# Second convolution product into FFN: a fixed order on every engine, two units' first products side by side, the sample's norms last

## The chip, the cores and the metric

The kernel runs on one core of a Trainium2 chip. The metric is the device time of one execution in microseconds (us).

## The reference, cut to what matters

One layer of an encoder, the same weights for a prompt of 1024 rows and a sample of 256 rows, all fp32, model width 1024, FFN width 2816:

```python
h = rms_norm(x, norms[0])
b, c, v = split(h @ conv_w_in, 3)
mix = (b * conv3(c * v)) @ conv_w_out        # the second product of the convolution
x = x + rms_norm(mix, norms[1])              # norm 1 and the residual
h = rms_norm(x, norms[2])                    # norm 2
gate, up = split(h @ ffn_w_in, 2)
x = x + rms_norm((silu(gate) * up) @ ffn_w_out, norms[3])
```

## The kernel before, in words

**Arithmetic.** A matrix product in fp32 is made of three products of parts in fp32r: each operand is split into a high part (ScalarE, a copy that rounds) and a low part (VectorE, operand minus high part), and high x high, high x low and low x high are summed in PSUM (`TERMS`, `product`, L200). On top, the prompt's part of a product is done with Strassen-like sums of 2 x 2 blocks: seven block products of 12 matmuls each instead of eight.

**Stages.** First the input product of the convolution (12 units), then the second product, here called mm2 (weights `w2t`, result tiles `mx`), then FFN-in (22 units F0, F1, ..., each of 128 gate and 128 up columns), then FFN-out (weights `w4`). The 1280 rows make ten tiles of 128, 0 to 7 of the prompt and 8 and 9 of the sample; mm2 takes them in the order 0, 4, 1, 5, 2, 6, 3, 7, 8, 9.

**After a tile of mm2** (`after_mm2`, L683): ScalarE squares the two halves with a running sum, VectorE and GpSimd make the factor of norm 1, VectorE scales the two halves, adds the residual (`x1`), SP stores `x1` to DRAM, then the same again for norm 2 (squares, factor, one scaling into `ht`). Two tiles later TensorE transposes `ht` in two halves of four 128 x 128 blocks (`transposes`, L650). Prompt tiles go into the quadrants a11, a12, a21, a22 (`ar`), sample tiles are split into `hs`, high part on ScalarE and low part on VectorE.

**Operands of FFN-in.** `early_sums` (L711) splits a11 and forms the block sums (a21 + a22, then a11 minus that, then s3) for a range of columns; `make_c` splits a12, s1 (the a21 sum), s2 (the a11 sum), s3, a22 and s4 (a12 plus the a11 sum). A unit's weights are loaded as 1 MB (`load`, L162) and split as `g`, `u`, then `sums`, `t13`, `t24` (`make`, L177). A unit (`Block`, L210) does its block products in the order x: a11 with g; y: a12 with g; x: s2 with t24; z: s1 with t13; x: s3 with t13; the sample's two products (24 matmuls of 256 columns each); x: a22 with t24; z: s4 with u. The bank x is added to and read out several times, each time before its next product. `EvF` (L809) holds what is read out, its SiLU and the product with the up part.

**What sets the order.** Up to the end of FFN-in the instructions are put in order by the framework's scheduler, which follows the program's order as priority and runs ahead where operands and places are free. Here, F0's and F1's first instructions and the norms of tiles 8 and 9 are all in its hands. FFN-out is under `tc.manual_schedule()` (L1247): there each engine keeps the order in which the program names the instructions, chosen by a planner written out in the kernel (`fill`, `advance`, clocks in us for each engine, `row_free` for the time from which a buffer row is free). `load_w4` (L912) asks for the next 1 MB of FFN-out weights, into a place of pool `b` or into two rows of the pools `a` and `s`; `load_units` (L1042) asks for the activation tiles (`ut`, and the small ones `us` that the `yo` product reads). All of these loads, and the stores of `spill`, go out on SP's queue in order, and a load that must wait for its place holds those behind it. PSUM has eight banks, taken in turn.

Of the kernel before, what the change touches and what calls it, by code (L numbers as in the profile page):

```python
# [8 lines left out]
F32 = mybir.dt.float32  # L9
# [27 lines left out]
def encoder_kernel(ctx: ExitStack, tc: tile.TileContext, xT, x, g0T, gB, cwT, w1, w2, w3, w4, out_p, out_s):  # L37
# [3 lines left out]
    const = ctx.enter_context(tc.tile_pool(name="const", bufs=1))  # L41
    tmp = ctx.enter_context(tc.tile_pool(name="tmp", bufs=3))
    mem = ctx.enter_context(tc.tile_pool(name="mem", bufs=1))
    ps = ctx.enter_context(tc.tile_pool(name="ps", bufs=8, space=PS))
    dram = ctx.enter_context(tc.tile_pool(name="dram", bufs=1, space=bass.MemoryType.DRAM))


# [57 lines left out]
    def copy(out, a):  # L105
        nc.scalar.activation(out, a, AF.Copy)  # L106

    def new_ps(name):
        return ps.tile([P, 512], F32, tag="mm", name=name)

    def new_tmp(name):
        return tmp.tile([P, 512], F32, tag="ta", name=name, bufs=6)
# [9 lines left out]
    def sumsq(parts, name, i=None):  # L122

        acc = small(2, name)
        for h, src in enumerate(parts):
            junk = new_tmp(f"j_{name}_{h}")
            nc.scalar.activation(junk, src, AF.Square, accum_out=acc[:, h : h + 1])
        tot = small(1, name + "t")
        if i is None:
            add(tot, acc[:, 0:1], acc[:, 1:2])  # L130
        else:
            nc.vector.scalar_tensor_tensor(
                out=tot, in0=acc[:, 0:1], scalar=acc[:, 1:2], in1=rq[:, i : i + 1], op0=ALU.add, op1=ALU.mult
            )
        rstd(tot, tot, 1)
        if i is not None:
            nc.gpsimd.tensor_tensor(out=tot, in0=tot, in1=rt[:, i : i + 1], op=ALU.mult)
        return tot

    def halves(ap):  # L140
        return [ap[:, :H], ap[:, H:]]
# [502 lines left out]
    for i in (0, 1):  # L644
        nc.sync.dma_start(gb[:, i], gB[i].partition_broadcast(P))
    ar = {(kh, c): get(f"ar{kh}{c}", [KH, 512]) for kh in (0, 1) for c in (0, 1)}
    hs[:] = [get(f"hs{p}", [KD, 256], F32R) for p in "hl"]
    hts, mx = {}, {}

    def transposes(i):  # L650
        for q in range(2):
            o = new_ps(f"tr{i}_{q}")
            for k in range(4):
                nc.tensor.transpose(
                    o[:, k * P : (k + 1) * P], hts[i][:, (4 * q + k) * P : (4 * q + k + 1) * P], ident
                )
            ov = o.rearrange("p (k t) -> p k t", k=4)
            if i < 8:
                t0 = i % 4 * P
                dst = ar[q, i // 4][:, :, t0 : t0 + P]  # L660
                if q:
                    nc.vector.tensor_copy(dst, ov)
                else:
                    copy(dst, ov)
            else:
                t0 = (i - 8) * P
                split(*(h[:, 4 * q : 4 * q + 4, t0 : t0 + P] for h in hs), ov)
        put(hts.pop(i))

    def mm2(*tiles, ks=range(KD)):  # L670
        for i in tiles:
            if i not in mx:
                mx[i] = [new_ps(f"mx{i}_{h}") for h in range(2)]
# [9 lines left out]
    def after_mm2(i):  # L683
        put(zs.pop(i))
        xt = xts.pop(i)
        o = mx.pop(i)
        r = sumsq(o, f"n1_{i}", i)
        x1 = get(f"x1_{i}", [D], kind="a")
        for h in range(2):
            sl = slice(h * H, (h + 1) * H)  # L690
            nc.vector.scalar_tensor_tensor(
                out=x1[:, sl], in0=o[h], scalar=r, in1=gb[:, 0, sl], op0=ALU.mult, op1=ALU.mult
            )
        add(x1, x1, xt)
        put(xt)
        nc.sync.dma_start(x1d[i], x1)
        r = sumsq(halves(x1), f"n2_{i}")
        hts[i] = get(f"ht{i}", [D], kind="s")
        nc.vector.scalar_tensor_tensor(out=hts[i], in0=x1, scalar=r, in1=gb[:, 1], op0=ALU.mult, op1=ALU.mult)
        put(x1)  # L700

    xts = {}

# [17 lines left out]
        load_z(i, KD - 2, KD)  # L721
    for i in ORDER2[:2]:
        load_xt(i)
    for n, i in enumerate(ORDER2):
        last = n == NT - 1
        if n == 0:
            mm2(i, ORDER2[1])
        elif n > 1:
            if n == 8:
                load_z(ORDER2[9])  # L730
                cb["a11"] = [get(f"a11{p}", [KH, 512], F32R) for p in "hl"]
                s3 = get("s3", [KH, 512])
                early_sums(slice(0, 3 * P))
            early = KD - 2 if n < 4 else 1
            mm2(i, ks=range(early))
            transposes(ORDER2[n - 2])
            if last:
                early_sums(slice(3 * P, 4 * P))
            mm2(i, ks=range(early, KH))
            if last:  # L740
                put(*w2t[:KH])
                make_c("a12", a12)
                add(a12, a12, a11)
                make(F0, "t24")
                make_c("s2", a11)
                put(a11)
            mm2(i, ks=range(max(early, KH), KD))
        if last:
            put(*w2t[KH:])
        after_mm2(i)  # L750
        if n and not last:
            if n != 8:
                load_z(ORDER2[n + 1])
            load_xt(ORDER2[n + 1])
        if n == 4:
            load(F0)
            for what in ("g", "u", "sums"):
                make(F0, what)
    make(F0, "t13")
    make_c("s1", a21)  # L760
    put(a21)
    make_c("s3", s3)
    put(s3)


    A11, S1, S2, S4, A12, S3, A22 = range(7)
# [42 lines left out]
    class EvF:  # L809


        def __init__(self, f):
            self.f = f
            self.a = act[f] = get(f"act{f}", [2, HALF], kind="a")

        def tmp(self, q):
            return new_tmp(f"{q}{self.f}_")
# [4 lines left out]

        def add11(self, y):
            add(self.c11, self.c11, y)
            nc.scalar.activation(self.c11, self.c11, AF.Silu)

        def read12(self, x):
# [1 line left out]
            copy(self.c12, x)  # L829

        def read22(self, x, z):
            self.c22 = self.tmp("c22")
            copy(self.c22, x)
            add(self.c22, self.c22, z)

        def read21(self, x):
            g2 = self.tmp("g2")
            nc.scalar.activation(g2, x, AF.Silu)
            mul(prompt(self.a, 1), g2, self.c22)

        def add12(self, z):
            add(self.c12, self.c12, z)
# [7 lines left out]
        def end(self):  # L850
            pass

    def ffn_in(f):
        units = [("f", g) if g < KF else None for g in (f, f + 1, f + 2)]
        if f:
            b = Block(units[0], EvF(f), *units[1:], final=f == KF - 1)
            b.p12()
            b.p657()
            b.sample()
            b.p43()  # L860
        else:
# [12 lines left out]
            b.p657(after6)  # L874
            transposes(ORDER2[-2])
            transposes(ORDER2[-1])
            put(gb)
            make(F1, "u")
            make(F1, "sums")
            b.p43(lambda: make(F1, "t13"))  # L880
            b.sample()
            make(F1, "t24")
            load(F2)
        if f % 2 and f < KF - 1:
            for _ in spill(f // 2):
                pass
# [25 lines left out]
    def load_w4():  # L912
# [21 lines left out]
    def weights():  # L934

        for gi, grp in enumerate(GROUPS):
            for jn, j in enumerate(grp):
# [135 lines left out]
    def advance(entry, limit):  # L1073
# [2 lines left out]
            return False  # L1076
        ready = ready() if callable(ready) else ready or 0.0
        if rows:
            tags = (free["s"] + free["a"])[:rows]
            ready = max([ready] + [row_free.get(tag, 0.0) for tag in tags])  # L1080
        done = max(clock[engine], ready) + cost
        if done > limit:
            return False
# [249 lines left out]
```

## Time and profile before

| | us |
|---|---|
| median of 3 runs | 1273.21 (1272.68 to 1274.07) |
| the profiled execution | 1271.61 |
| its span, first to last instruction | 1269.8 |
| TensorE busy | 1242.1 (98%) |
| VectorE busy | 841.0 (66%) |
| ScalarE busy | 466.4 (37%) |
| mean granted TensorE clock | 0.993 of full |

The profiled execution's time is 1.8 us more than its span: what lies before the first and after the last instruction. Busy shares are means over all stages; a matmul counts as busy until its modelled end, so neighbours overlap. mm2 runs from 323.5 to 440.1 us, FFN-in from there to 996.0, FFN-out after that.

### The profile page before, as it was taken

The numbers are of one execution on the slowest core, as the hardware profiler recorded it, in microseconds if no ns is written. First come the engines' busy times: TensorE is split into PE (matmuls) and PEld (weight loads), VectorE is DVE, ScalarE is ACT, GpSimd is POOL, SyncE is SP. The second block draws the span as 40 slices with busy tenths as digits, with TensorE's granted clock in tenths as the row PEclk, the third lists the DMA queues.
The fourth block names the chain that finished last, engine by engine and source line by source line (L and its number), as shares of the span: only waits on it lengthen the run. The fifth ranks groups of instructions, "written<-read, shape, count | busy, mean of one in ns | idle before, by whom it ended". The sixth has DMA issues, their size and how long they took to land.

```text
span 1269.8 us, 15906 instructions
## 1 busy us (share of the span) xinstructions
PE 1242.1 (98%) x6213; PEld 1052.6 (83%) x6213; DVE 841.0 (66%) x1177; ACT 466.4 (37%) x694; POOL 26.5 (2%) x49
## 2 busy tenths in 40 slices
PE   8899999999999989999999999999999999999997
PEld 6688888888888868888888888888888878788885
DVE  7996655757265786565664755755657478769566
ACT  7743332325133554333343433433434342112011
POOL 0100000000011100000000000000000000000000
PEclk9899999999999999999999999999999999999999
DMA  7504041225953213452552642634626788866894
GB/s 266 165 34 149 34 117 54 87 92 175 336 204 124 103 49 109 129 170 97 157 158 87 178 128 85 189 113 120 191 86 196 268 284 295 277 225 209 284 331 176
DMA packets 185595, 207.37 MB, mean 163 GB/s; under 512 B 7984, under 2 KB 145584, under 8 KB 184496
## 3 DMA queue, kind: packets, MB, share of 16 engines
q1 hardware_dynamic: 185088, 205.83, 50.0%
q8 instruction: 49, 0.80, 0.3%
q10 hardware_dynamic: 432, 0.53, 0.1%
q14 instruction: 26, 0.21, 0.0%
HBM read 134.89 MB, written 71.43 MB: 162 GB/s over the span
## 4 chain that ended last, share of the span: by engine, by line
PE 88%; DVE 5%; DMA 3%; issue 1%; ACT 1%; POOL 1%; SPq 1%; POOLq 0%; DVEq 0%; ACTq 0%
PE xo L1132 11%; PE zo L1132 5%; PE mx L678 4%; PE yo L1132 3%; DMA us<-actd 1%; PE xf__6682 L204 1%; PE xf__3760 L204 1%; PE xp__710 L204 1%; PE xf__7635 L204 1%; PE xf__7456 L204 1%; PE xf__7243 L204 1%; PE xf__7069 L204 1%; PE xf__6856 L204 1%; PE xf__5521 L204 1%; PE xf__5308 L204 1%
## 5 line engine op out<-in xcount | busy, mean ns | idle before, releaser
L678 PE MATMUL mx<-w2s,zs 128*128 128x512 f32 x480 | 111.1, 391 | 0.0
L678 PEld LDWEIGHTS mx<-w2s,zs 128*128 128x128 f32 x480 | 89.5, 188 | 18.2
L106 ACT ACTIVATE st<-act 128x640 fp32r<-128x640 f32 x77 | 56.8, 738 | 92.4 <-DMA actd<-st 59.5
L100 DVE TENSOR_TENSOR y<-y,xo 128x512 f32<-128x512 f32 x85 | 58.4, 687 | 28.3 <-PE xo L1132 27.8
L97 DVE TENSOR_TENSOR st<-act,st 128x640 fp32r<-128x640 f32 x77 | 63.3, 822 | 17.8 <-ACT st L106 17.0
L1132 PE MATMUL xo<-w4t,us 128*128 128x512 f32 x273 | 68.9, 389 | 0.0
L1132 PEld LDWEIGHTS xo<-w4t,us 128*128 128x128 f32 x273 | 51.3, 188 | 10.7
L1132 PE MATMUL xo<-w4t,ut 128*128 128x512 f32 x222 | 55.4, 389 | 0.0
L106 ACT ACTIVATE w4t<-w4r 128x1024 fp32r<-128x1024 f32 (+1 forms) x23 | 23.5, 1024 | 70.0 <-DVE w4r L97 58.0
L1132 PEld LDWEIGHTS xo<-w4t,ut 128*128 128x128 f32 x222 | 41.7, 188 | 8.6
L100 DVE TENSOR_TENSOR y<-y,zo 128x512 f32<-128x512 f32 x45 | 30.9, 687 | 19.9 <-PE zo L1132 19.5
L1132 PE MATMUL zo<-w4t,ut 128*128 128x512 f32 x165 | 41.7, 390 | 0.0
L1132 PE MATMUL xo<-w4b,ut 128*128 128x512 f32 x165 | 41.6, 390 | 0.0
L1132 PE MATMUL zo<-w4b,ut 128*128 128x512 f32 x165 | 41.5, 389 | 0.0
L1164 ACT ACTIVATE junk<-y 128x1024 f32<-128x1024 f32 (+1 forms) x12 | 11.0, 918 | 73.7 <-DVE y L100 72.4
L1132 PEld LDWEIGHTS zo<-w4t,ut 128*128 128x128 f32 x165 | 31.0, 188 | 6.7
L1132 PEld LDWEIGHTS xo<-w4b,ut 128*128 128x128 f32 x165 | 31.0, 188 | 6.5
L1132 PEld LDWEIGHTS zo<-w4b,ut 128*128 128x128 f32 x165 | 31.0, 188 | 6.4
L1132 PE MATMUL yo<-w4b,us 128*128 128x512 f32 x114 | 29.2, 391 | 2.4 <-DMA us<-actd 2.4
L414 DVE SCALAR_TENSOR_TENSOR row<-u,cw,row 128x256 f32<-128x256 f32 (+1 forms) x32 | 28.1, 882 | 4.1 <-ACT row L412 3.9
L106 ACT ACTIVATE w4b<-w4r 128x512 fp32r<-128x512 f32 (+1 forms) x22 | 18.1, 839 | 33.4 <-DMA us<-actd 12.5
L97 DVE TENSOR_TENSOR w4t<-w4r,w4t 128x1024 fp32r<-128x1024 f32 (+1 forms) x23 | 26.9, 1175 | 1.2 <-ACT w4t L106 1.2
(2120 smaller groups left out, 3357.1 us busy)
## 6 DMA issues: line engine op xcount, KB each, us to landing
actd<-st SPq DMA_DIRECT2D x154, 320.0 KB, 2.8
ut<-actd SPq DMA_DIRECT2D x20, 1024.0 KB, 7.6
us<-actd SPq DMA_DIRECT2D x62, 256.0 KB, 5.2
ut<-actd SPq DMA_DIRECT2D x16, 768.0 KB, 7.8
zd<-zst SPq DMA_DIRECT2D x32, 320.0 KB, 3.1
zs<-zd SPq DMA_DIRECT2D x8, 1024.0 KB, 6.4
w4r<-w SPq DMA_DIRECT2D x11, 512.0 KB, 4.6
w4r<-w SPq DMA_DIRECT2D x22, 256.0 KB, 4.6
```

Source lines behind the costliest of these rows:

```text
L97: nc.vector.tensor_tensor(out=out, in0=a, in1=b, op=ALU.subtract)
L100: return nc.vector.tensor_tensor(out=out, in0=a, in1=b, op=ALU.add)
L106: nc.scalar.activation(out, a, AF.Copy)
L204: nc.tensor.matmul(out[:, :n], stat(w, k), mov(part, k), start=first and k == 0 and j == 0, stop=last and k == KH - 1 and j == 2, skip_gro ...
L414: nc.vector.scalar_tensor_tensor(out=out, in0=src, scalar=cw[:, j, dd : dd + 1], in1=out, op0=ALU.mult, op1=ALU.add)
L678: nc.tensor.matmul(mx[i][h], zs[i][:, part, k], w2t[k][:, w, h * H : (h + 1) * H], start=k == 0 and j == 0, stop=k == KD - 1 and j == 2,)
L1132: nc.tensor.matmul(acc, stat[n, c, j][:, ap], w[wp], start=starts and jn == 0 and m == 0, stop=jn == len(grp) - 1 and m == 2, skip_group_c ...
L1164: nc.scalar.activation(junk, src, AF.Square, accum_out=acc[:, col : col + 1])
```

## The change

The ten tiles of mm2 are no longer one loop. Tiles up to 7 stay in it; there, the sums over the first two column ranges and the splits of all of F0's weights are asked for. Tiles 8 and 9 of mm2, F0 whole and F1's first two products are one function, `entry`, under `tc.manual_schedule()`. In it, `after_mm2` is taken apart into six steps (`norm_squares`, `norm_factor`, `norm_residual`, `norm_squares2`, `norm_factor2`, `norm_end`, with the instructions of before) that are named one by one between the others; the low part of `hs` is made by a later call (`take_left`); F1's first two products come right behind F0's first two; each PSUM bank is named. `EvF` is cut into smaller steps (`silu11`, `copy22`, `silu21`) and takes its row when it first writes it. In FFN-out, `load_w4` loads into rows only when the planner's clock has passed the time from which they are free, and the end of a weight's last split is entered as that time.

```diff
-    ps = ctx.enter_context(tc.tile_pool(name="ps", bufs=8, space=PS))
+    ps = ctx.enter_context(tc.tile_pool(name="ps", bufs=1, space=PS))
...
-    def new_ps(name):
-        return ps.tile([P, 512], F32, tag="mm", name=name)
+    turn = [0]
+    def new_ps(name, bank=None):
+        if bank is None:
+            bank = turn[0] % 8
+            turn[0] += 1
+        return ps.tile([P, 512], F32, tag=f"bank{bank}", name=name)
...
-    hs[:] = [get(f"hs{p}", [KD, 256], F32R) for p in "hl"]
...
-                split(*(h[:, 4 * q : 4 * q + 4, t0 : t0 + P] for h in hs), ov)
+                copy(hs[0][:, 4 * q : 4 * q + 4, t0 : t0 + P], ov)
+                left.append((i, q, ov))
...
+    left = []
+    def take_left():
+        while left:
+            i, q, ov = left.pop(0)
+            t0 = (i - 8) * P
+            h, l = (h[:, 4 * q : 4 * q + 4, t0 : t0 + P] for h in hs)
+            sub(l, ov, f32(h))
...
+    MX_BANKS = {(8, 0): 4, (8, 1): 5, (9, 0): 2, (9, 1): 3}
...
-    for n, i in enumerate(ORDER2):
-        last = n == NT - 1
+    for n, i in enumerate(ORDER2[:8]):
         if n == 0:
             mm2(i, ORDER2[1])
         elif n > 1:
-            if n == 8:
-                load_z(ORDER2[9])
-                cb["a11"] = [get(f"a11{p}", [KH, 512], F32R) for p in "hl"]
-                s3 = get("s3", [KH, 512])
-                early_sums(slice(0, 3 * P))
             early = KD - 2 if n < 4 else 1
             mm2(i, ks=range(early))
             transposes(ORDER2[n - 2])
-            if last:
-                early_sums(slice(3 * P, 4 * P))
-            mm2(i, ks=range(early, KH))
-            if last:
-                put(*w2t[:KH])
-                make_c("a12", a12)
-                add(a12, a12, a11)
-                make(F0, "t24")
-                make_c("s2", a11)
-                put(a11)
-            mm2(i, ks=range(max(early, KH), KD))
-        if last:
-            put(*w2t[KH:])
+            mm2(i, ks=range(early, KD))
+            if n == 4:
+                cb["a11"] = [get(f"a11{p}", [KH, 512], F32R) for p in "hl"]
+                s3 = get("s3", [KH, 512])
+                early_sums(slice(0, P))
+            if n == 6:
+                early_sums(slice(P, 2 * P))
         after_mm2(i)
-        if n and not last:
-            if n != 8:
-                load_z(ORDER2[n + 1])
+        if n:
+            load_z(ORDER2[n + 1])
             load_xt(ORDER2[n + 1])
         if n == 4:
             load(F0)
             for what in ("g", "u", "sums"):
                 make(F0, what)
-    make(F0, "t13")
-    make_c("s1", a21)
-    put(a21)
-    make_c("s3", s3)
-    put(s3)
+        if n == 6:
+            for what in ("t24", "t13"):
+                make(F0, what)
...
+    second = []
+    def parts_of(name, src):
+        cb[name] = [get(f"{name}{p}", [KH, 512], F32R) for p in "hl"]
+        hi, lo = cb[name]
+        def high(k):
+            copy(hi[:, k : k + 2], src[:, k : k + 2])
+        def low(k):
+            sub(lo[:, k : k + 2], src[:, k : k + 2], f32(hi[:, k : k + 2]))
+        return high, low
+    def both(step):
+        step(0)
+        step(2)
+    def entry():
+        load_z(9)
+        load(F1)
+        early_sums(slice(2 * P, 3 * P))
+        mm2(8, ks=range(1))
+        transposes(ORDER2[6], (6, 7))
+        mm2(8, ks=range(1, KD))
+        norm_squares(8)
+        load_xt(9)
+        mm2(9, ks=range(1))
+        put(w2t[0])
+        transposes(ORDER2[7], (0, 1))
+        norm_factor(8)
+        for k in range(1, KD):
+            mm2(9, ks=range(k, k + 1))
+            put(w2t[k])
+        early_sums(slice(3 * P, 4 * P))
+        high, low = parts_of("a12", a12)
+        both(high)
+        both(low)
+        make(F1, "g")
+        high, low = parts_of("s2", a11)
+        both(high)
+        both(low)
+        e0, e1 = EvF(0), EvF(1)
+        b0 = Block(F0, e0, banks={q: new_ps(f"{q}f0_", b) for q, b in (("x", 6), ("y", 7))})
+        b1 = Block(F1, e1, F2, ("f", 3), banks={q: new_ps(f"{q}f1_", b) for q, b in (("x", 0), ("y", 1))})
+        b0.run("x", "g", 0, "a11", True)
+        b0.run("y", "g", 1, "a12", True)
+        b1.run("x", "g", 0, "a11", True)
+        b1.run("y", "g", 1, "a12", True)
+        high, low = parts_of("s1", a21)
+        both(high)
+        norm_squares(9)
+        norm_residual(8)
+        e0.read11(b0.bank["x"])
+        both(low)
+        put(a21)
+        norm_squares2(8)
+        norm_factor(9)
+        add(e0.c11, e0.c11, b0.bank["y"])
+        high, low = parts_of("s3", s3)
+        both(high)
+        norm_factor2(8)
+        norm_residual(9)
+        norm_end(8)
+        e1.read11(b1.bank["x"])
+        norm_squares2(9)
+        add(e1.c11, e1.c11, b1.bank["y"])
+        both(low)
+        put(s3)
+        high, low = parts_of("a22", a22)
+        both(high)
+        norm_factor2(9)
+        e0.silu11()
+        b0.run("x", "t24", 0, "s2", False)
+        e0.read12(b0.bank["x"])
+        e1.silu11()
+        b0.bank["z"] = new_ps("zf0_", 4)
+        b0.run("z", "t13", 0, "s1", True)
+        both(low)
+        put(a22)
+        hs[:] = [get("hsh", [KD, 256], F32R)]
+        transposes(8, (5, 2))
+        b0.run("x", "t13", 1, "s3", False)
+        b0.drop("t13")
+        add(a12, a12, a11)
+        put(a11)
+        hs.append(get("hsl", [KD, 256], F32R))
+        norm_end(9)
+        put(gb)
+        high, low = parts_of("s4", a12)
+        high(0)
+        e0.copy22(b0.bank["x"])
+        high(2)
+        both(low)
+        put(a12)
+        take_left()
+        add(e0.c22, e0.c22, b0.bank["z"])
+        transposes(9, (3, 5))
+        b0.run("x", "t24", 1, "a22", False)
+        b0.drop("t24")
+        take_left()
+        e0.read21(b0.bank["x"])
+        b0.run("z", "u", 1, "s4", False)
+        make(F1, "u")
+        make(F1, "sums")
+        e0.add12(b0.bank["z"])
+        make(F1, "t24")
+        b0.bank.update(sg=new_ps("sgf0_", 7), su=new_ps("suf0_", 2))
+        b0.half = True
+        b0.sample()
+        make(F1, "t13")
+        b1.bank.update({q: new_ps(f"{q}f1_", b) for q, b in (("z", 6), ("sg", 3), ("su", 5))})
+        turn[0] = 7
+        load(F2)
+        return b1
     def ffn_in(f):
         units = [("f", g) if g < KF else None for g in (f, f + 1, f + 2)]
-        if f:
+        if f == 0:
+            with tc.manual_schedule():
+                second.append(entry())
+        elif f == 1:
+            b = second[0]
+            for what in ("g", "u", "sums"):
+                make(F2, what)
+            b.p657()
+            b.sample()
+            b.p43()
+        else:
             b = Block(units[0], EvF(f), *units[1:], final=f == KF - 1)
             b.p12()
             b.p657()
             b.sample()
             b.p43()
-        else:
-            b = Block(F0, EvF(0))
-            def after6():
-                make_c("a22", a22)
-                put(a22)
-                make_c("s4", a12)
-                put(a12)
-                make(F1, "g")
-            b.p12()
-            load(F1)
-            b.p657(after6)
-            transposes(ORDER2[-2])
-            transposes(ORDER2[-1])
-            put(gb)
-            make(F1, "u")
-            make(F1, "sums")
-            b.p43(lambda: make(F1, "t13"))
-            b.sample()
-            make(F1, "t24")
-            load(F2)
...
+    def rows_ready(n):
+        return max([row_free.get(tag, 0.0) for tag in (free["s"] + free["a"])[:n]])
...
-        elif rows_free() >= 2 + bool(act_left):
+        elif rows_free() >= 2 + bool(act_left) and rows_ready(2) <= clock["pe"]:
             parts = [get(f"w4r{j}{h}", [2, 512], kind="as") for h in (0, 1)]
             raw4[j] = (*parts, parts)
...
-                yield "dve", 1.16, done2, 0, 0, gi
+                done = yield "dve", 1.16, done2, 0, 0, gi
                 sub(t24[:, 1], rb, f32(t24[:, 0]))
+                for t in rows:
+                    row_free[held[id(t)][1]] = done
                 put(*rows)
```

## Rows read from the trace of the kernel before

**Rows 1.** The page, busy time of each engine.

```profile
PE 1242.1 (98%) x6213; PEld 1052.6 (83%) x6213; DVE 841.0 (66%) x1177; ACT 466.4 (37%) x694; POOL 26.5 (2%) x49
```

**Rows 2.** Timeline of TensorE, 440 to 481 us: start, length, instruction, idle time before.

```profile
440.10 0.39 PE L204 MATMUL xf__3543<-a11h,wgf__3032 128*128 128x512 f32 x1
...
446.75 0.50 PE L204 MATMUL zf__3545<-s1h,wt13f__3527 128*128 128x512 f32 x1 [1.05 <-ACT wt13f__3527 L93]
...
451.37 0.50 PE L204 MATMUL zf__3545<-s1l,wt13f__3527 128*128 128x512 f32 x1 [1.71 <-DVE s1l L94]
...
454.35 0.80 PE L204 MATMUL xf__3543<-s2h,wt24f__3468 128*128 128x512 f32 x1 [1.56 <-ACT c__3560 L106]
...
459.63 0.50 PE L204 MATMUL xf__3543<-s3h,wt13f__3527 128*128 128x512 f32 x1 [0.69 <-ACT c__3591 L106]
...
480.16 0.39 PE L204 MATMUL xf__3760<-s2h,wt24f__3753 128*128 128x512 f32 x1
```

**Rows 3.** Chain of waits, 415 to 482 us: start, length, what, instructions.

```profile
454.35 4.61 PE xf__3543 L204 x12
...
462.67 0.87 PE tr L654 x8
...
471.98 2.88 PE suf__3547 L204 x24
...
477.61 2.72 PE yf__3761 L204 x12
```

**Rows 4.** Busy time by stretch: window, length, engines, granted clock, DMA share, GB/s.

```profile
440.00:475.00 35.00, 30.00 (x152) 24.55 (x151) 31.67 (x38) 20.48 (x31) 3.10 (x3) 0.95 0.16 56
...
34.00:42.00 8.00, 7.20 (x21) 5.21 (x20) 8.00 (x8) 7.35 (x13) 0.00 (x0) 0.57 0.70 198
...
454.30:458.00 3.70, 3.65 (x9) 2.97 (x10) 3.26 (x6) 3.22 (x4) 1.46 (x1) 0.54 0.07 27
```

**Rows 5.** Timeline of TensorE, FFN-out, the two waits.

```profile
1040.87 1.66 PE L1132 MATMUL yo<-w4b,us 128*128 128x512 f32 x6 [1.16 <-DMA us<-actd]
...
1080.53 1.66 PE L1132 MATMUL yo<-w4b,us 128*128 128x512 f32 x6 [1.26 <-DMA us<-actd]
```

**Rows 6.** Chain of waits, FFN-out, the first of two such pieces.

```profile
1031.97 8.86 DMA us<-actd
```

**Rows 7.** Waits of the SP queue, 995 to 1100 us: total, times, longest.

```profile
SPq L931 <- DMA actd<-st: 10.1, 2, 5.3
```

**Rows 8.** Timeline of the SP queue around the change.

```profile
422.92 0.32 SPq L696 DMA_DIRECT2D x1d<-x  x1
```

**Rows 9.** Timeline of ScalarE around the change.

```profile
428.30 0.60 ACT L127 ACTIVATE j_n<-mx 128x512 f32<-128x512 f32 x1 [4.03 <-PE mx L678]
...
457.66 1.05 ACT L93 ACTIVATE s4h<-ar 128x1024 fp32r<-128x1024 f32 x1
...
458.98 0.60 ACT L106 ACTIVATE c__3591<-xf__3543 128x512 f32<-128x512 f32 x1 [0.28 <-PE xf__3543 L204]
```

**Rows 10.** Tile zs: landing of its ten loads.

```profile
DMA to landing us min/median/max: 3.0/5.7/11.1
```

**Rows 11.** Timeline of VectorE around the change.

```profile
439.92 2.28 DVE L100 TENSOR_TENSOR ar<-ar,ar 128x2048 f32<-128x2048 f32 x1
...
442.12 1.22 DVE L94 TENSOR_TENSOR wt24f__3468<-wrf__3029,wt24f__3468 128x1024 fp32r<-128x1024 f32 x1
...
452.37 2.35 DVE L94 TENSOR_TENSOR s3l<-s,s3h 128x1024 fp32r<-128x1024 f32 x2
...
454.70 0.68 DVE L100 TENSOR_TENSOR c__3560<-c__3560,yf__3544 128x512 f32<-128x512 f32 x1
...
457.02 1.28 DVE L699 SCALAR_TENSOR_TENSOR ht<-x,n_9t,gb 128x1024 f32<-128x1024 f32 x1 [0.44 <-POOL n_9t L117]
```

**Rows 12.** Timeline of TensorE at the kernel's start.

```profile
33.57 0.50 PE L204 MATMUL xc__149<-s2l,wt24p__322 128*128 128x512 f32 x1 [2.88 <-DVE s2l L94]
```

**Rows 13.** The page, DMA issues: count, KB each, us to landing.

```profile
w4r<-w SPq DMA_DIRECT2D x11, 512.0 KB, 4.6
```

More of the change, by code (lines that the diff above doesn't have):

```diff
@@ L120, in small, with squares_of @@
         return tmp.tile([P, 4], dt, tag="small", name=name, bufs=8)[:, :n]
-    def sumsq(parts, name, i=None):
+    def squares_of(parts, name):
         acc = small(2, name)
@@ L127, in sumsq, with factor @@
             nc.scalar.activation(junk, src, AF.Square, accum_out=acc[:, h : h + 1])
+        return acc
+    def factor(acc, name, i=None):
         tot = small(1, name + "t")
@@ L646, in encoder_kernel, with transposes @@
     ar = {(kh, c): get(f"ar{kh}{c}", [KH, 512]) for kh in (0, 1) for c in (0, 1)}
-    hs[:] = [get(f"hs{p}", [KD, 256], F32R) for p in "hl"]
     hts, mx = {}, {}
-    def transposes(i):
+    def transposes(i, banks=(None, None)):
         for q in range(2):
-            o = new_ps(f"tr{i}_{q}")
+            o = new_ps(f"tr{i}_{q}", banks[q])
             for k in range(4):
@@ L672, in mm2 @@
             if i not in mx:
-                mx[i] = [new_ps(f"mx{i}_{h}") for h in range(2)]
+                mx[i] = [new_ps(f"mx{i}_{h}", MX_BANKS.get((i, h))) for h in range(2)]
         for k in ks:
@@ L681, in mm2, with norm_squares, norm_factor, norm_residual @@
                         )
-    def after_mm2(i):
+    MX_BANKS = {(8, 0): 4, (8, 1): 5, (9, 0): 2, (9, 1): 3}
+    factors, x1s = {}, {}
+    def norm_squares(i):
         put(zs.pop(i))
[L685 to L688, printed above, removed]
+        factors[i] = squares_of(mx[i], f"n1_{i}")
+    def norm_factor(i):
+        factors[i] = factor(factors[i], f"n1_{i}", i)
+    def norm_residual(i):
+        xt, o = xts.pop(i), mx.pop(i)
+        x1 = x1s[i] = get(f"x1_{i}", [D], kind="a")
         for h in range(2):
@@ L691, in after_mm2 @@
             nc.vector.scalar_tensor_tensor(
-                out=x1[:, sl], in0=o[h], scalar=r, in1=gb[:, 0, sl], op0=ALU.mult, op1=ALU.mult
+                out=x1[:, sl], in0=o[h], scalar=factors[i], in1=gb[:, 0, sl], op0=ALU.mult, op1=ALU.mult
             )
@@ L696, in after_mm2, with norm_squares2, norm_factor2, norm_end @@
         nc.sync.dma_start(x1d[i], x1)
-        r = sumsq(halves(x1), f"n2_{i}")
+    def norm_squares2(i):
+        factors[i] = squares_of(halves(x1s[i]), f"n2_{i}")
+    def norm_factor2(i):
+        factors[i] = factor(factors[i], f"n2_{i}")
+    def norm_end(i):
+        x1 = x1s.pop(i)
         hts[i] = get(f"ht{i}", [D], kind="s")
-        nc.vector.scalar_tensor_tensor(out=hts[i], in0=x1, scalar=r, in1=gb[:, 1], op0=ALU.mult, op1=ALU.mult)
+        nc.vector.scalar_tensor_tensor(
+            out=hts[i], in0=x1, scalar=factors[i], in1=gb[:, 1], op0=ALU.mult, op1=ALU.mult
+        )
         put(x1)
+    def after_mm2(i):
+        for step in (norm_squares, norm_factor, norm_residual, norm_squares2, norm_factor2, norm_end):
+            step(i)
     xts = {}
@@ L813, in __init__, with a @@
             self.f = f
-            self.a = act[f] = get(f"act{f}", [2, HALF], kind="a")
+        @property
+        def a(self):
+            if self.f not in act:
+                act[self.f] = get(f"act{self.f}", [2, HALF], kind="a")
+            return act[self.f]
         def tmp(self, q):
@@ L824, in add11, with silu11 @@
             add(self.c11, self.c11, y)
+            self.silu11()
+        def silu11(self):
             nc.scalar.activation(self.c11, self.c11, AF.Silu)
@@ L831, in read22, with copy22, silu21 @@
         def read22(self, x, z):
+            self.copy22(x)
+            add(self.c22, self.c22, z)
+        def copy22(self, x):
             self.c22 = self.tmp("c22")
             copy(self.c22, x)
-            add(self.c22, self.c22, z)
         def read21(self, x):
-            g2 = self.tmp("g2")
-            nc.scalar.activation(g2, x, AF.Silu)
-            mul(prompt(self.a, 1), g2, self.c22)
+            self.silu21(x)
+            mul(prompt(self.a, 1), self.g2, self.c22)
+        def silu21(self, x):
+            self.g2 = self.tmp("g2")
+            nc.scalar.activation(self.g2, x, AF.Silu)
         def add12(self, z):
@@ L1078, in advance @@
         if rows:
-            tags = (free["s"] + free["a"])[:rows]
-            ready = max([ready] + [row_free.get(tag, 0.0) for tag in tags])
+            ready = max(ready, rows_ready(rows))
         done = max(clock[engine], ready) + cost
```

## The prediction, made before the changed kernel ran

> **What bounds the kernel now.** I read the page first: TensorE is busy for 98% of the span [rows 1], so only its idle time and its slow stretches can be won. Next the TensorE timeline around the change, for the times at which it waits. The first product of F0 starts at 440.10 and the third product of F1 at 480.16, 40.06 us later [rows 2]. The chain of waits gives the work in between: nine products of 2.72 (seven of F0, two of F1), two sample products of 2.88, two times eight transposes at 0.87 [rows 3]. That is 24.48 + 5.76 + 1.74 = 31.98 us, so 8.1 us of this stretch are lost. Four waits of 1.05, 1.71, 1.56 and 0.69 us [rows 2] are 5.0 of it. A matmul is shown 0.39 long but follows its neighbour by 2.72 / 12 = 0.23, so each wait costs 0.16 more than its idle time: 0.6. Another 1.9 is the product after the third wait, which took 4.61 us where 2.72 is usual [rows 3]: the granted clock of that stretch was 0.54, so mostly the 1.2 GHz level [rows 4]. The last 0.6 is slower refilling after the waits. The same group shows VectorE busy for 31.7 of the 35 us from 440 to 475 [rows 4]: what the waits end on is its queue, and ScalarE behind it.
>
> Two more waits stand in FFN-out, of 1.16 and 1.26 us before a `yo` product [rows 5]; with 0.16 each they cost 2.7. The chain names the small activation tile, the first time 8.86 us under way [rows 6]. The waits of the SP queue say why it was late: the second part of a `w4r` load (line 931) waited twice, 10.1 us in all, for a store out of its row [rows 7], and everything behind it on SP waited too.
>
> **The change, part by part.** Everything is counted in the profiled execution's time (1271.6 us, span 1269.8), and set on the median at the end. No matmul, transpose, split or norm is added or removed.
>
> *Load of tile 9.* It becomes the first instruction of the fixed part, so on SP it stands behind the store of tile 7's `x1`, issued at 422.92 [rows 8]. Tile 8's products end at 428.3, where its squares start [rows 9], and then tile 9's are wanted. A 1 MB load of this kind lands in 3.0 to 11.1 us, 5.7 in the middle [rows 10]: with 0.32 and 0.38 of issue, between 426.6 and 434.7, so TensorE waits 0 to 6.4 us. I take 0: the store itself should come about 1 us sooner, because the 1536-wide sums that now stand in VectorE's queue during tile 7's norm are cut into 512-wide pieces, most of them done earlier. That leaves 428.3 by the middle figure. F1's weights (1 MB) are issued right behind. The Trainium skill (DMA: Bandwidth & Descriptors, section on queues, rings and completion order) says that each DMA engine takes descriptors in ring order; by that rule F1's load costs tile 9's nothing, and if the two shared the engines instead, the landing would move from the 5.7 toward the 11.1. No row here separates the two.
>
> *F1's first two products before F0's third.* They are 5.44 us of work that needs only a11, a12 and F1's gate weights. Their price is one split of weights earlier, 1.06 on ScalarE and 1.14 on VectorE; F0's two summed splits (2.3 on each) leave the stretch in exchange. In the written order VectorE does the remaining sums, a12, F1's split, s2, tile 8's residual and s1 by about 444.6, then F0's y, tile 9's residual and tile 8's last norm step by 450.5, just before F1's y product ends at 451.2 (440.10 + 4 x 2.72 + the last matmul's tail). So all the old waits, on s1, F0's summed weights and the reads of x, are covered, with 0.7 to spare on VectorE.
>
> *What is late next.* After F1's y, VectorE's order is: that PSUM add, s3, a factor of tile 9, a22, the 2048-wide a12 sum, tile 9's last norm step, s4, and only then the low part of tile 8's first transposed half. The rows give 0.68, 2.35 for two splits, 2.28 and 1.28 [rows 11]; an instruction starts 0.08 before the shown end of the one ahead (439.92 + 2.28, and the next at 442.12). So 0.60 + 2.27 + 0.26 + 2.27 + 2.20 + 1.20 + 2.27 + 0.68 = 11.8 us, until 463.0. ScalarE adds 0.6: s4's second high part (1.05) stands behind the copy of x (0.60) [rows 9], which waits for the s3 product's end at 460.2. So it is done at 463.6. TensorE meanwhile has s2, s1, tile 8's transposes, s3 and half of tile 9's transposes: 3 x 2.72 + 0.87 + 0.43 = 9.5 us from 450.98, until 460.4. Its next four transposes go into bank 5, which also holds tile 8's first half, and must wait for that low part. So one wait of **3.2 us** takes the place of the four. It would be 0 if VectorE ran ahead by as much, which the order forbids as far as I can see (the add of F1's y is its anchor); the upper end is 6, if the chain before the anchor is later than I count.
>
> *The clock after it.* At the kernel's start a wait of 2.88 us [rows 12] was followed by 8 us at a clock of 0.57; in the transition three waits of 4.3 us together were followed by 0.54 [rows 4]. So I charge one product at half clock, 1.9, and 0.2 of refilling; the bounds are 0 and 3.4 (8 x 0.43). The Trainium skill (TensorE: Matmul & The Clock Gate, section on what is actually happening) says that the gate follows how busy the array has been of late; by that rule a gap in one piece counts as one in four does, as charged, while if only repeated gaps were punished the time would be 1.9 lower.
>
> *After that.* F1's u, sums and t24 parts are some 9.5 us of VectorE, ready by 473.5; TensorE wants t24 at 477. F2's load goes out about 3 us later than now and is wanted five products and a sample pair later, 19 us. Both are covered.
>
> Entry: 8.1 lost now, 3.2 + 0.2 + 1.9 = 5.3 lost then, **2.8 won** (8.1 at most; below nothing if the long wait passes 6).
>
> *Rows ready before a `w4r` load.* The planner now refuses a load into rows whose last use isn't over by its clock. That takes away the blocking of [rows 7]: the small tiles go out when asked, up to 5 us sooner, and land before `yo` wants them. **2.7 won** (at most that; below nothing if a load then comes too late, a rival below). A group of two is 5 x 7 products of six matmuls, 47.6 us, and the loads put off are for the group after the next, so some 40 us lie between.
>
> Sum: 2.8 + 2.7 = 5.5. From 1271.6 that gives 1266.1; the median of the runs, 1273.2, stands 1.6 above the profiled execution, so **1267.7**.
>
> **The rivals.**
> - *The clock stays up* after the one wait: 1267.7 - 1.9 = 1265.8. For it: three of the old waits came before the clock fell, and one piece might not do it. Against: this wait is longer than the 2.88 that did.
> - *No long wait*: VectorE frees bank 5 in time and the entry loses nothing: 1273.2 - 8.1 - 2.7 = 1262.4. For it: VectorE still has 3.3 idle us of 35 [rows 4] that an order without holes could use. Against: the anchor, F1's y, comes after them.
> - *The guard does nothing*: the planner's estimate of when a row is free runs ahead of the store, so SP blocks as now: 1270.4, the entry as forecast. For it: the estimate is a formula.
> - *The entry gains nothing*: VectorE is 3 us later at its anchor (tile 9's or F1's load lands late and holds the queues), the long wait grows to 6, and the small tiles meet the loads that were put off. About 1273.
> - *Slower*: the guard puts off a `w4r` load until a group begins without its weights. Then TensorE waits for the landing, 4.6 [rows 13], and for VectorE's five 512-wide and three 1024-wide instructions on the tile, 5 x 0.60 + 3 x 1.14 = 6.4: 11.0 lost against 5.5 won, 1278.7. It decides once the refusals add up to more than the 40 us of slack; against it, each ends when a store lands, some 5 us by [rows 7].
>
> **How the numbers follow.** Forecast 0.40, clock stays 0.14, no long wait 0.18, guard idle 0.12, entry gains nothing 0.08, slower 0.08. Less than 0.2% (2.5 us) can't be told from no change here: the border is 1270.7, and half of the guard's case lies on either side. Faster 0.40 + 0.14 + 0.18 + 0.06 = 0.78, same 0.06 + 0.08 = 0.14, slower 0.08. The range takes in the first four cases (0.84): 1261.8 to 1272.0.
>
> **What would show it.** No TensorE wait before F0's third product and no 1.2 GHz there; F1's x and y products between F0's y and its s2 product. One wait inside tile 9's transposes, released by VectorE's low part of `hs`, of about 3 us, and a slow product behind it. F1's third product starting near 477 instead of 480.2. No `us` wait at `yo` in FFN-out, and no wait of line 931's successor for a store. The prediction is wrong if tile 9's first product waits for its load, if the wait on bank 5 is missing, or if a group in FFN-out begins with a wait for `w4` weights.

## The result, and the profile after

| | before | after |
|---|---|---|
| median of 6 runs, us | 1273.64 (1272.68 to 1274.86) | **1267.87** (1265.93 to 1268.14) |
| ratio, 95% interval | | 0.995 (0.9937 to 0.9963) |
| profiled execution, its span | 1271.61, 1269.8 | 1265.93, 1264.2 |
| mean granted clock | 0.993 | 0.992 |

The change made the kernel 5.8 us faster; 1267.7 was predicted. To see whether the parts agree too, I cut both profiles at five instructions of the TensorE timeline: the first product of mm2, F0's first product, F1's `s2` product (its third), the first and the last `xo` group of FFN-out.

| stage, us | before | after | difference | forecast |
|---|---|---|---|---|
| start and second convolution | 323.53 | 321.69 | -1.84 | 0 |
| mm2 | 116.57 | 117.25 | +0.68 | 0 |
| entry (F0 to F1's third product) | 40.06 | 37.56 | -2.50 | -2.8 |
| rest of FFN-in | 515.87 | 516.87 | +1.00 | 0 |
| FFN-out | 263.16 | 260.12 | -3.04 | -2.7 |

Both terms that I forecast came in by size; that the second one did is partly luck, as e3 shows below. The rest is three shifts in stages that the change was not aimed at; they sum to -0.2, which is luck.

**The entry.** The TensorE timeline of after, 440 to 477 us (start, length, instruction, idle time before and its releaser), answers to [rows 2]: tile 8's eight transposes, the only two rows with an idle time, what follows them, and F1's third product.

```profile
455.27 1.03 PE L662 MATMUL tr<-ident,ht 128*128 128x128 f32 x8
...
459.38 0.65 PE L662 MATMUL tr<-ident,ht 128*128 128x128 f32 x4 [0.35 <-DVE ht L733]
463.47 1.12 PE L662 MATMUL tr<-ident,ht 128*128 128x128 f32 x4 [3.44 <-DVE hsl L97]
464.24 0.78 PE L213 MATMUL xf__3503<-a22h,wt24f__3237 128*128 128x512 f32 x1
...
468.02 0.40 PE L213 MATMUL zf__3633<-s4h,wuf__3041 128*128 128x512 f32 x1
...
476.50 0.40 PE L213 MATMUL xf__3505<-s2h,wt24f__3739 128*128 128x512 f32 x1
```

The four old waits are gone. One long wait stands inside tile 9's eight transposes, between the fourth and the fifth, released by VectorE's low part of `hs`. The chain of waits of after says what led there (start, length, what), and answers to [rows 3]:

```profile
459.07 1.06 ACT s4h L106
460.13 0.48 ACT c__3680 L106
460.61 0.95 ACT s4h L106
461.57 0.02 issue
461.59 1.22 DVE s4l L97
462.81 0.61 DVE hsl L97
463.43 0.04 issue
463.47 1.12 PE tr L662 x4
464.59 3.59 PE xf__3503 L213 x12
468.18 2.73 PE zf__3633 L213 x12
```

Read it backwards: the transposes wait for `hsl`, that one stands behind `s4l`, that one waits for ScalarE's second half of `s4h`, which stands behind the copy of x. The product after the wait takes 3.59 us where 2.73 follows. VectorE's timeline of after shows the same queue, with its idle times (it answers to [rows 11]):

```profile
450.44 0.69 DVE L100 TENSOR_TENSOR c__3599<-c__3599,yf__3506 128x512 f32<-128x512 f32 x1 [1.05 <-PE yf__3506 L213]
451.05 2.35 DVE L97 TENSOR_TENSOR s3l<-s,s3h 128x1024 fp32r<-128x1024 f32 x2
...
455.84 2.28 DVE L100 TENSOR_TENSOR ar<-ar,ar 128x2048 f32<-128x2048 f32 x1
458.05 1.28 DVE L733 SCALAR_TENSOR_TENSOR ht<-x,n_9t,gb 128x1024 f32<-128x1024 f32 x1
460.16 1.23 DVE L97 TENSOR_TENSOR s4l<-ar,s4h 128x1024 fp32r<-128x1024 f32 x1 [0.84 <-ACT s4h L106]
461.59 1.22 DVE L97 TENSOR_TENSOR s4l<-ar,s4h 128x1024 fp32r<-128x1024 f32 x1 [0.20 <-ACT s4h L106]
462.73 1.28 DVE L97 TENSOR_TENSOR hsl<-tr,hsh 128x512 fp32r<-128x512 f32 x2
```

Busy time by stretch in after (columns as in [rows 4]): the same 35 us, the wait, and what follows it.

```profile
440.00:475.00 35.00, 31.21 (x157) 26.25 (x156) 28.80 (x37) 17.90 (x31) 2.73 (x4) 0.95 0.08 31
459.30:463.40 4.10, 0.65 (x4) 0.42 (x4) 3.06 (x5) 2.75 (x4) 0.00 (x0) 0.93 0.00 0
463.40:466.80 3.40, 3.33 (x11) 2.87 (x12) 2.50 (x5) 0.60 (x1) 0.00 (x0) 0.58 0.02 5
```

**FFN-out.** No wait of TensorE answers to [rows 5]: the waits view of after has none between 985 us and the end. What took its place on SP (timeline of the SP queue) is not what I had in mind:

```profile
1017.19 0.46 SPq L1076 DMA_DIRECT2D w4r<-w  x1
1017.70 0.90 SPq L1078 DMA_DIRECT2D w4r<-w  x2
1018.72 0.43 SPq L1076 DMA_DIRECT2D w4r<-w  x1
1019.25 1.51 SPq L1078 DMA_DIRECT2D w4r<-w  x2
1023.37 1.22 SPq L807 DMA_DIRECT2D actd<-st  x2
```

The second of these loads stands directly behind the first, ahead of the next spill stores (`actd<-st`). In before it stood behind the spill, and its second part (line 931) is the one that waited in [rows 7] (timeline of the SP queue of before):

```profile
1021.39 1.77 SPq L782 DMA_DIRECT2D actd<-st  x2
1023.52 1.17 SPq L929 DMA_DIRECT2D w4r<-w  x1
1029.54 0.82 SPq L931 DMA_DIRECT2D w4r<-w  x2
```

So the load went earlier, not later; only the sixth load of the stage went later, from 1070.42 to 1082.42.

**The stages I had at 0.** In the convolution the order of two products changed. Two idle times of TensorE in before, between 56 and 59 us:

```profile
56.68 0.50 PE L204 MATMUL xv__150<-s2h,wt24p__507 128*128 128x512 f32 x1 [1.41 <-ACT wt24p__507 L93]
58.39 1.22 PE L204 MATMUL xv__150<-s2h,wt24p__507 128*128 128x512 f32 x2 [0.98 <-DVE wt24p__507 L94]
```

and of after, at the same place:

```profile
57.97 0.74 PE L213 MATMUL zv__157<-s1h,wt13p__536 128*128 128x512 f32 x2 [0.92 <-DVE wt13p__536 L94]
```

All waits of TensorE that the view of waits lists before mm2 add up to 11.3 us in before and 10.1 in after, so they hold 1.2 of the 1.84.

In the rest of FFN-in after has one wait that before has not (view of waits, 476 to 990 us: total, times, longest), and in mm2 two (321 to 440 us), where before has 0.3:

```profile
PE xf__6307 L213 <- ACT c__6362 L106: 0.8, 1, 0.8
```

```profile
PE tr L662 <- DVE ht L733: 0.6, 1, 0.6
PE tr L662 <- DVE n_4t L141: 0.3, 1, 0.3
```

### The profile page after: what moved, and what is told of

Same layout as the page of the kernel before. It is cut to its first block, busy times and chain, and to the rows that moved or that the text cites. A ratio compares the mean times of both kernels' runs of the same rounds, so it can differ in the third digit from the quotient of the medians.

```text
span 1264.2 us, 15922 instructions
## 1 busy us (share of the span) xinstructions
PE 1239.7 (98%) x6213; PEld 1052.3 (83%) x6213; DVE 842.0 (67%) x1185; ACT 465.8 (37%) x696; POOL 25.4 (2%) x49
## 4 chain that ended last, share of the span: by engine, by line
PE 90%; DVE 5%; DMA 2%; ACT 1%; issue 1%; POOL 1%; SPq 0%; POOLq 0%; DVEq 0%; ACTq 0%
PE xo L1280 12%; PE zo L1280 6%; PE mx L696 5%; PE yo L1280 3%; DMA wrf__3035<-w 1%; PE xf__3503 L213 1%; PE xp__710 L213 1%; PE xf__3505 L213 1%; PE xf__3985 L213 1%; PE xf__7468 L213 1%; PE xp__1456 L213 1%; PE xf__7255 L213 1%; PE xf__7081 L213 1%; PE xf__6868 L213 1%; PE xf__6694 L213 1%; PE xf__5920 L213 1%
## 5 line engine op out<-in xcount | busy, mean ns | idle before, releaser
L1280 PEld LDWEIGHTS xo<-w4t,us 128*128 128x128 f32 x273 | 51.2, 188 | 10.7
```

What stands on the lines that cost most here:

```text
L1280: nc.tensor.matmul(acc, stat[n, c, j][:, ap], w[wp], start=starts and jn == 0 and m == 0, stop=jn == len(grp) - 1 and m == 2, skip_group_c ...
```

## The experiments

Ratios are to the kernel before, run on the same chip, with 95% intervals. The later runs of before scatter more (1270 to 1283), and the profile shown of it (1271.6) lies 2.4 to 3.3 us under their medians of 1274 to 1275. Single stages scatter too: in the four profiles whose kernel is that of before up to FFN-out (before, e2, e5, e6), mm2 takes 116.55 to 118.17 us and the entry 40.04 to 41.24. So a difference of about 1 us in one of these stages says nothing by itself.

**e1_bank: the long wait alone.** Tile 9's second four transposes go into a bank that nobody holds.

```diff
-        transposes(9, (3, 5))
+        transposes(9, (3, 7))
...
-        b0.bank.update(sg=new_ps("sgf0_", 7), su=new_ps("suf0_", 2))
+        b0.bank.update(sg=new_ps("sgf0_", 5), su=new_ps("suf0_", 2))
...
-        b1.bank.update({q: new_ps(f"{q}f1_", b) for q, b in (("z", 6), ("sg", 3), ("su", 5))})
-        turn[0] = 7
+        b1.bank.update({q: new_ps(f"{q}f1_", b) for q, b in (("z", 6), ("sg", 3), ("su", 7))})
+        turn[0] = 2
```

> The changed kernel with the second half of tile 9's transposes in bank 7 instead of bank 5 (and the sample's banks of F0 and F1 exchanged to suit). Theory, the one long wait of the entry is the bank alone: the 3.4 us wait and the slow product behind it (3.59 instead of 2.72) go, 4.5 us; but F1's summed weights are then the next late thing, since VectorE needs 7.4 us from the end of F0's a22 product until they are split, against 8.5 of TensorE work, so up to 1.5 comes back: 1263.4 to 1265. Rival, the low part of hs is late itself and the wait only moves to the sample's products behind it: 1267 to 1268.

Measured: 1262.62, ratio 0.9907 (0.989 to 0.9924). TensorE's idle times in the entry (timeline):

```profile
459.52 1.09 PE L662 MATMUL tr<-ident,ht 128*128 128x128 f32 x8 [0.36 <-DVE ht L733]
460.79 0.50 PE L213 MATMUL xf__3503<-a22h,wt24f__3237 128*128 128x512 f32 x1 [0.18 <-ACT c__3680 L106]
...
464.79 0.50 PE L213 MATMUL zf__3633<-s4h,wuf__3041 128*128 128x512 f32 x1 [0.99 <-DVE c__3680 L100]
```

The eight transposes now run in one piece, and the granted clock stays up (busy time by stretch, the stretch where after had 0.58 and the 35 us):

```profile
440.00:475.00 35.00, 33.47 (x176) 28.09 (x175) 31.30 (x40) 19.35 (x33) 2.73 (x4) 1.00 0.15 57
...
463.40:466.80 3.40, 2.41 (x11) 1.67 (x10) 3.40 (x7) 1.55 (x2) 0.00 (x0) 1.00 0.02 5
```

The entry takes 34.34, 3.2 less than after, and the span 3.4 less. By the medians it is 5.3 less; after's profile was the fastest of its six runs. That shows that bank 5 was the cause and that the lower clock came with the wait. The wait that I expected at F1's summed weights did not come (their split ended at 472.9, wanted at 473.4); one of 0.99, on an addition that stands behind the same low parts, came instead. With nothing given back there, the median lies 0.8 under the range that I expected.

**e2_guard_only, e5_refuse_only, e6_entry_only: the guard and its two halves, each put into the kernel before.** The guard has two edits. e5 has only the first (without the entry, the free time of a row comes from the spill stores alone), e6 only the second, e2 both.

```diff
-        elif rows_free() >= 2 + bool(act_left):
+        elif rows_free() >= 2 + bool(act_left) and rows_ready(2) <= clock["pe"]:
...
-                yield "dve", 1.16, done2, 0, 0, gi
+                done = yield "dve", 1.16, done2, 0, 0, gi
                 sub(t24[:, 1], rb, f32(t24[:, 0]))
+                for t in rows:
+                    row_free[held[id(t)][1]] = done
```

> The kernel before with only the guard on loads into rows in FFN-out. Theory, the guard removes both waits for the small tiles: 2.7 to 3.0 us less than before, 1270.6 to 1270.9, no wait at yo. Rival, the gain in FFN-out came from the other order in which the rows are taken, and the guard refuses nothing that matters: 1273.6, both waits as before.

> The kernel before, with only the refusal in the guard (a load into rows waits until the planner's clock passes the rows' free time), without the new entry of that time after a weight's last split. In its order the fourth weight load of FFN-out stands some three units later on SP. Theory of the prediction, the refusal itself frees SP: both waits at yo gone, 263.2 us of FFN-out become 260.1 to 260.5, 3 us less than before. Rival, the refusal isn't what helped: over 262.

> The kernel before, with only the entry of the free time after a weight's last split, and no refusal. Its order on SP around the two waits is that of the whole guard: a load stands ahead of the store that it waited for, because the spill's next part now waits for the row. Rival of the prediction, this entry alone does it: FFN-out 260.1 to 260.5 us as with the whole guard, 3 us less than before. Theory of the prediction (the refusal): no change, 263 us.

| | median | ratio | FFN-out | waits at `yo` |
|---|---|---|---|---|
| e2, both | 1270.81 | 0.9968 (0.9952 to 0.9984) | 260.13 | none |
| e5, refusal | 1270.22 | 0.9968 (0.9953 to 0.9984) | 259.76 | none |
| e6, entry | 1271.73 | 0.9975 (0.9959 to 0.9992) | 260.13 | none |

Each half alone is enough to take the two waits away; by the medians the three save 2.3 to 4.1 us, and FFN-out is 3.0 to 3.4 shorter. In e5 a load is really put off until behind the spills (timeline of SP):

```profile
1023.08 1.93 SPq L782 DMA_DIRECT2D actd<-st  x2
1026.11 3.07 SPq L782 DMA_DIRECT2D actd<-st  x2
...
1033.97 4.21 SPq L782 DMA_DIRECT2D actd<-st  x2
...
1040.70 1.22 SPq L782 DMA_DIRECT2D actd<-st  x2
1043.13 0.89 SPq L932 DMA_DIRECT2D w4r<-w  x1
```

In e6 nothing is refused, and SP's order around the two waits is that of e2 and after; further on one load stands a few issues earlier (1084.5, in e2 1087.8). By the planner's text, with the free time entered, it makes the spill wait for its row, and the load takes the rows that are free already. So the refusal that I reasoned with works, but in the change it was the entry that set the order there.

**e3_no_guard: the change without the guard.** Both edits above taken out of the changed kernel.

```diff
-        elif rows_free() >= 2 + bool(act_left) and rows_ready(2) <= clock["pe"]:
+        elif rows_free() >= 2 + bool(act_left):
...
-                for t in rows:
-                    row_free[held[id(t)][1]] = done
```

> The changed kernel without the guard. Theory: the second part of a row load waits for a store again, the small tiles are late, 2.7 to 3.0 us more: 1270.6 to 1270.9. Rival, the rows order alone: 1267.9.

Measured: 1270.3, ratio 0.9964 (0.995 to 0.9978). FFN-out takes 261.13, 1.0 more than after. The waits of SP and of TensorE from 985 us on:

```profile
SPq L1078 <- DMA actd<-st: 10.2, 2, 5.2
```

```profile
PE yo L1278 <- DMA us<-actd: 0.4, 1, 0.4
```

SP is blocked for as long as before (10.1), yet TensorE loses 0.4 instead of 2.4. So in the profiles the guard is worth 1.0 in the changed kernel (the stage repeats well: 260.12 or 260.13 in after, e1, e2, e6, e7 and e8), where I expected 2.7 to 3.0, and 3.0 in before; the medians don't settle it, as the intervals of e3 and after overlap (0.995 to 0.9978 and 0.9937 to 0.9963). e4 below, also without a guard, has 261.57. So some 2 of the 3.0 us by which FFN-out got shorter came without the guard. What the same blocking costs presumably hangs on when `yo` wants its tiles; that was not tested, and why e3 and e4 differ from before stays open.

**e4_banks_only: only the bank rule in the kernel before.** The pool of eight becomes eight names taken in turn; nothing else changes.

```diff
-    ps = ctx.enter_context(tc.tile_pool(name="ps", bufs=8, space=PS))
+    ps = ctx.enter_context(tc.tile_pool(name="ps", bufs=1, space=PS))
...
+    turn = [0]
     def new_ps(name):
-        return ps.tile([P, 512], F32, tag="mm", name=name)
+        bank = turn[0] % 8
+        turn[0] += 1
+        return ps.tile([P, 512], F32, tag=f"bank{bank}", name=name)
```

> The kernel before with only its PSUM banks named in a fixed turn instead of taken from a pool of eight. In the two profiles the stage before the second convolution product, whose text is the same, was 1.8 us shorter after the change. Theory, the named banks give the scheduler another order there: that stage again 1.5 to 2 us shorter than before, 1271.6 to 1272.1. Rival, it is the scatter of single executions: 1273.6, the stage within 0.5 of before in its order and length.

Measured: 1271.59, ratio 0.9981 (0.9966 to 0.9996). Its stages are 321.67, 117.51, 41.70, 516.48 and 261.57. So the shifts in the first and the fourth stage (-1.9, +0.6) come with the names alone; mm2's +0.9 lies inside its scatter. The entry is 1.6 longer than in before (0.5 above its scatter) and FFN-out 1.6 shorter. Over all profiles, the four with the pool need 323.5 to 325.4 for the convolution, the six with names 320.2 to 322.3; for FFN-in 515.8 to 515.9 against 516.5 to 516.9. In e4 too the products at 57 us are those of after, with one wait of 0.94. Why the scheduler sorts them otherwise when the banks have names I did not find out.

**e8_not_beside: F1's first two products back behind F0's sample pair.** The rest of the fixed order stays, and F1's reads of x and y and its SiLU move with them.

```diff
-        b1.run("x", "g", 0, "a11", True)
-        b1.run("y", "g", 1, "a12", True)
...
         b0.sample()
+        b1.run("x", "g", 0, "a11", True)
+        b1.run("y", "g", 1, "a12", True)
```

> The changed kernel with F1's first two products moved back behind F0's sample products, all else in its fixed order. Theory, those 5.44 us of work cover the norms of tiles 8 and 9: without them TensorE waits about 1 us for s3, about 3 for tile 9's last norm step and again about 3 for bank 5, 7 in all against 4 now, and the clock falls for longer: 3 to 5 us more than the changed kernel, 1271 to 1273. Rival, the fixed order and the earlier F0 weights do it and the side by side is incidental: within 1 us of the changed kernel, 1267 to 1269.

Measured: 1271.95, ratio 0.9979 (0.9964 to 0.9994), 4.1 more than after by the medians; the entry takes 42.81, 5.25 more. TensorE's waits there, and a row of ScalarE ahead of the first:

```profile
456.13 0.80 PE L213 MATMUL xf__3503<-s3h,wt13f__3240 128*128 128x512 f32 x1 [3.13 <-ACT c__3603 L106]
...
465.08 0.66 PE L662 MATMUL tr<-ident,ht 128*128 128x128 f32 x4 [4.00 <-DVE hsl L97]
...
450.41 0.63 ACT L132 ACTIVATE j_n<-x 128x512 f32<-128x512 f32 x1 [2.64 <-DVE x L100]
```

The size was as the first theory had it; the place of the first wait was not (ScalarE's read of x, not VectorE's norm of tile 9). The norm stands behind it all the same: that read comes after tile 9's squares, which waited 2.64 for VectorE's residual, a22's high part, a table load of 1.28 (at 453.66) and F0's SiLU. The two products are what covers the stretch; the fixed order without them is no better than the old loop (42.81 against 40.04 to 41.24).

**e7_reordered: e1, and the order on VectorE and ScalarE mended.** Tile 9's last norm step goes before the 2048-wide sum, the copy of x and the addition of `z` before `s4`, both tiles' low parts of `hs` behind the transposes with the first halves first, and F1's `t24` split ahead of F0's last additions; the product with the SiLU of the last read (`mul`) moves behind that split.

```diff
-        add(a12, a12, a11)
-        put(a11)
-        hs.append(get("hsl", [KD, 256], F32R))
         norm_end(9)
         put(gb)
+        add(a12, a12, a11)
+        put(a11)
+        hs.append(get("hsl", [KD, 256], F32R))
...
-        high(0)
         e0.copy22(b0.bank["x"])
-        high(2)
+        add(e0.c22, e0.c22, b0.bank["z"])
+        both(high)
         both(low)
         put(a12)
-        take_left()
-        add(e0.c22, e0.c22, b0.bank["z"])
         transposes(9, (3, 7))
         b0.run("x", "t24", 1, "a22", False)
         b0.drop("t24")
+        left.sort(key=lambda e: e[1])
         take_left()
-        e0.read21(b0.bank["x"])
+        e0.silu21(b0.bank["x"])
         b0.run("z", "u", 1, "s4", False)
         make(F1, "u")
         make(F1, "sums")
-        e0.add12(b0.bank["z"])
         make(F1, "t24")
+        mul(prompt(e0.a, 1), e0.g2, e0.c22)
+        e0.add12(b0.bank["z"])
```

> The kernel of e1_bank with four steps moved: tile 9's last norm step ahead of the wide a12 sum, the copy and the sum of the up part ahead of s4's parts, the low parts of hs in the order in which the sample's products read them, and F1's weights ahead of the two activation products. In e1_bank the entry still waits 0.36, 0.18 and 0.99 us, 2.0 with the tails. Theory, VectorE's order is what is left: those go, at most 0.5 comes back at F1's summed weights, 1.5 to 2.0 less than e1_bank, 1260.6 to 1261.1. Rival, ScalarE's s4 parts are late by themselves (they now stand behind the copy): the wait moves to s4, 1262 to 1262.8.

Measured: 1261.49, ratio 0.9897 (0.9871 to 0.9922), the lowest median of all, 0.4 above the range that I expected. TensorE has no idle time in the stretch and its clock is full:

```profile
440.00:475.00 35.00, 35.00 (x187) 30.05 (x186) 30.63 (x39) 20.78 (x35) 2.73 (x4) 1.00 0.15 61
```

The entry takes 32.11, against 31.98 us of work counted in the prediction. Against e1 the entry is 2.2 shorter and the median only 1.1: in mm2 its profile waits 2.5 for a tile's norm, where e1's waits 1.4 and after's 0.3, though the three have the same text there. Intervals overlap, so e7 against e1 is not settled by the times.

## Why the prediction came out right, and where it didn't

*F1's first two products cover the old waits.* Right: no wait before tile 9's transposes, and e8 shows that these two products do it. The anchor held: VectorE was ahead by 1.05 when F1's y product ended, where I had 0.7.

*One wait on bank 5.* Right in place, cause and size: 3.44 idle, 3.66 with the restart (459.38 to 463.47, less 0.43 for four transposes), against 3.2. I had left out a smaller wait on the same path, 0.35 for tile 9's `ht`, which costs 0.5 by the 0.16 of each wait.

*The clock after it.* Right in kind, too large in size: 2.1 charged, 1.4 lost. (The fifth transpose starts at 463.47 and `z` at 468.02, 4.55 apart; four transposes and a product at the usual pace are 0.43 + 2.72 = 3.15.) The granted clock was 0.58 over 3.4 us, so mostly the 1.2 GHz level, and the product after that one took the usual 2.73. The Trainium skill (TensorE: Matmul & The Clock Gate, section on what is actually happening) says that the gate follows how busy the array was of late; the runs agree in so far as the one wait of 3.44 lowered the clock and e1, whose longest wait is 0.99, kept it at 1.00.

So the entry lost 3.66 + 0.5 + 1.4 = 5.6 where 5.3 was forecast: errors of +0.5, +0.5 and -0.7. The rival in which the clock stays up and the one without a long wait are out.

*After that.* Covered, as forecast, but only just. F1's `t24` was to be ready by 473.5, with 3.5 us to spare; VectorE ended its split at 476.32 (timeline), and the product that needs it started at 476.50.

```profile
475.10 1.22 DVE L94 TENSOR_TENSOR wt24f__3739<-wrf__3339,wt24f__3739 128x1024 fp32r<-128x1024 f32 x1
```

*The load of tile 9.* The price, 0, was right; the step was wrong. I put it behind the store of tile 7's `x1`. The SP timeline of after has it 17 us ahead of that store, and F1's weights too:

```profile
403.81 0.32 SPq L628 DMA_DIRECT2D zs<-zd  x1
...
415.59 0.56 SPq L182 DMA_DIRECT2D wrf__3339<-w  x1
...
421.22 0.33 SPq L722 DMA_DIRECT2D x1d<-x  x1
```

The fixed order holds among the instructions of `entry` only; what was written ahead of it is still threaded in between by the scheduler. So the load had more than 20 us before tile 9's products, and the 0 to 6.4 that I bounded was never in play. The Trainium skill's rule of ring order (DMA: Bandwidth & Descriptors, section on queues, rings and completion order), on which I weighed F1's load, was not tested: with loads that early no run here shows the difference.

*The guard.* FFN-out got 3.0 shorter, against 2.7, and the two waits went, but that the size fits is partly luck and the mechanism only half right. In the changed kernel the guard is worth 1.0 (e3); the other 2.0 came without it. And it worked by the entry, not by the refusal that I reasoned with (e5, e6). The rival in which loads come too late is out; neither after nor e5 has a wait of TensorE in FFN-out.

*What I had not in the sum.* The naming of the banks, which I read as part of the fixed order, also moved instructions in stages that the change wasn't aimed at: -1.84 in the first and +1.00 in the fourth. mm2's +0.68 is inside its scatter. All three are larger than my error in the entry, 0.3. That they cancel to -0.2, and that FFN-out got shorter by about what I had put on the guard, is why the total came within 0.2 us.

## What to carry to other kernels

When several short waits are replaced by a fixed order, list for every accumulator bank who reads it last and when: the wait that was left hung on one bank, and other bank numbers alone took 3.4 us off the span (1264.2 to 1260.8). Work that needs only what is ready (here the next unit's first products) can cover a transition that a fixed order of the late work alone did not (e8). And a change of how buffers are named can change the schedule everywhere: compare all stages, not the edited one, and take a part out again before it is credited with its stage (e3).

## What the runs showed of the hardware

Blocking of an in-order queue has no fixed price. SP stood still for 10.1, 10.2 and 10.7 us in before, e3 and e4, each time in two waits of a `w4r` load for the spill's stores; TensorE's idle time from it was 2.4, 0.4 and 0.8. Another 10.0 us for VectorE's `w4t`, in two waits of after, came with no wait of TensorE at all.

One GpSimd step, the power of a 128x1 factor, took 0.54 us at 444.25 and 1.46 at 453.74 in after, on the same tile shape (spans on GpSimd are rough in this profile). VectorE was busy for 0.53 of the 1.10 us around the first and for all of the 1.60 around the second. That VectorE's load is the cause was not tested.
